# Where the weights of the 256-column products begin inside their tiles

## The chip, the cores and the metric

The kernel runs on one core of a Trainium2 chip. The metric is device time in microseconds of one execution, as the median of three runs; the two versions are compared by that time. The profile is of one further execution, recorded by the hardware profiler.

## What is computed

The reference is a two-layer trunk over 512 tokens of width 1024, with 256 memory tokens. Layer 0 mixes tokens by forgetting attention and differential attention, layer 1 by an mLSTM; each is followed by cross-attention to the memory and by a gated ConvFFN of inner width 2816. All is float32. The parts that matter here are the matrix products:

```python
def memory_cross_attention(xn, memn, wq, wkv, wo):
    q = split_heads(xn @ wq, XATTN_HEADS)
    k, v = jnp.split(memn @ wkv, 2, axis=-1)
...
def conv_ffn(xn, w_up, conv_w, conv_b, w_down):
    h = causal_depthwise_conv(xn @ w_up, conv_w) + conv_b
    g, u = jnp.split(h, 2, axis=-1)
    return (jax.nn.gelu(g) * u) @ w_down
...
    return rms_norm(x, final_norm)
```

## The kernel before

Activations stand transposed: a tile holds 128 features on the partitions and the 512 tokens along the free dimension. To keep float32 precision, each operand is split in two float32r parts, a high part (names ending in h: `xh`, `wh`, `ah`) made by ScalarE, and the rest (`xl`, `wl`, `al`) made by VectorE. One product of 128x128 weights with the columns is then three matmuls, `mm3` (lines 289 to 294): high weights on high columns (L292), high weights on low columns (L293), low weights on high columns (L294). Each matmul loads its own 128x128 weights first (the PEld rows of the profile) and then streams its columns.

Two widths of product occur. A wide one streams all 512 tokens. A narrow one streams 256 columns, and there are three kinds of it that take their weights from the tiles in question:

- The up-projection of the FFN (`seven`, for 21 of the 22 pairs of gate and value blocks in each layer) and the queries of the cross-attention (`p_query`, 4 per layer) are done by a scheme that replaces eight half products by seven, p1 to p7, each of four 128x128 weight blocks on 256 columns, so 84 matmuls for one pair. Their weights are `wh` and `wl` (sets f3 and f1, made by `parts`) and the smaller tiles `s2`, `s4`, `a22`, in which the high part takes 512 columns and the low part the next 512. Their columns come from `xh`/`xl` or from the sums kept in the `kv` tiles (`T1` to `T4`).
- The keys of the cross-attention (`p_proj` with n=MEM, and `p_fill`) stream the 256 memory tokens, tiles `mem`.
- The last three blocks of the last down-projection (`finish`, `part`) are done in two halves of 256 tokens each, so that the final norm of the first half can begin early. Their columns are `ah`/`al`.

A weight tile is 1088 columns wide for 1024 columns of weights, so the weights can begin up to 64 columns (256 bytes) into it. Where they begin is set by `OFF` for the narrow products, `parts(off)`:

```python
        return [self.til(self.wp, tag, (P, 1088), F32R, bufs=3)[:, off : off + 1024] for tag in ("wh", "wl")]
```

`OFF` is 16 columns, 64 bytes. The wide products of most projections begin at 0. The down-projection's wide products (`down`, through `block`) use `OFF` too, since their columns `ah`/`al` stand 64 bytes further than `xh`, `xl`, `kv` and `mem` do: the tile pools begin with pads (`pad`), and modulo 256 bytes the built program places `xh`, `xl`, `kv`, `mem` and the weight tiles at 96, and `ah`/`al` at 160. `finish` calls `weight` without an offset, so its weights begin at 0. The value projection with n=256 (`p_proj_tok`) has the roles exchanged: there the weight tile is what is streamed, and it begins 48 columns in; it is not touched.

Where a wide `down` or `plain` block is followed by a narrow product, the last 128 columns of its `wl` are put a further 16 columns in (32 for `plain` in layer 1): `d["step"]`, `b["step"]` and `low` in `block`. These steps are not touched either.

The order of the instructions is set by two planners, `Plan` (attention, memory, queries) and `Sched` (the FFN), from written-in costs. Neither looks at offsets, and TensorE takes its instructions in that order.

Of the kernel before, what the change touches and what calls it, by code (L numbers as in the profile page):

```python
# [17 lines left out]
P = 128  # L18
# [7 lines left out]
LAST = len(CHUNKS) - 1  # L26
# [12 lines left out]
PARTS = 3  # L39
BIG = 1e30  # L40

OFF = 16
BANKS = {"s": ("s", 2), "b": ("s", 2), "w": ("w", 2), "t": ("w", 2)}

FOX_Q, FOX_K, FOX_V, FOX_F, DIF_Q, DIF_K, DIF_V = 0, 512, 1024, 1536, 1544, 2056, 2568
# [21 lines left out]
class Plan:  # L67
# [11 lines left out]
    def add(self, fn, dur=0.0, deps=(), prio=None, take=(), free=(), chain=(), pre=(), after=0.0, order=(), load=(), st=None):  # L79
        it = Item(fn, dur, [d for d in deps if d is not None], len(self.items) if prio is None else prio, take, free, chain, pre, after, order, load, st)  # L80
        it.n = len(self.items)
        self.items.append(it)
        return it
# [154 lines left out]
class Builder:  # L238
# [868 lines left out]
    def p_fill(self, pl, layer, after, prio, blocks):  # L1107

        self.fills = []
        for b in range(blocks):  # L1110
            st = {}
            last = None
            for m in (2 * b, 2 * b + 1):
                for k in range(0, KB8, 4):

                    def fn(m=m, k=k, st=st):
                        if k == 0:
                            st["w"] = self.weight(self.t["xk"][layer, m], off=OFF)
                            if m % 2 == 0:
# [67 lines left out]
    def p_query(self, pl, layer, h, order):  # L1187
# [6 lines left out]
        def wide(tag, raw):  # L1194
            both = self.til(self.kp, tag, (P, 1088), F32R, bufs=1)
            s = st[tag] = [both[:, c : c + 512] for c in (OFF, OFF + 512)]
            self.split(*s, raw)
# [11 lines left out]
        def p1():  # L1209
# [5 lines left out]
            if h == 1:  # L1215
                self.rest_load(layer, 1)
            st["f3"] = self.parts(OFF)
            self.split(*st["f3"], st["raw"][:])
# [7 lines left out]
        def p5():  # L1226
            st["f1"] = self.parts(OFF)
            self.split(*st["f1"], self.sums[h][:])
            st["R"] = self.bank("s")
            product(st["f1"], 512, T1, "R", True, range(4 - (h == 0)))  # L1230
# [67 lines left out]
    def xattn(self, layer):  # L1298
        nc, t, tc = self.nc, self.t, self.tc
        with tc.tile_pool(name=f"xa{layer}", bufs=1, reuse_waits="tile") as mp:  # L1300
# [78 lines left out]
            for h in range(4):  # L1379
                p = 50 + 10 * h  # L1380
                ke = []
                for m in (2 * h, 2 * h + 1):
# [7 lines left out]
                    if m < 2 * len(self.fills):  # L1390
# [9 lines left out]
                        self.p_proj(  # L1400
                            pl, t["xk"][layer, m], self.mems, keys, kc, deps=[kvs], prio=p, n=MEM, per=4, off=OFF
                        )
# [118 lines left out]
    def ffn_steps(self, layer, mp):  # L1521
# [19 lines left out]
        def joined(deps, prio, free):  # L1541
            return add("-", 0.0, None, deps, prio, (), free, 0.0)
# [41 lines left out]
        def block(src, nk, xs, at, bank, deps, steps, tag="raw", off=0, onto=None):  # L1584

            st, lo = weight(src, nk * P, at, tag, off)
            last = None
            per = nk // steps

            def opened():  # L1590
                st["ps"] = self.bank(bank) if bank == "w" else self.acc_bank(st["_acc"] if bank == "acc" else 2 + st["_y"])

            if onto is not None:
                x, x_deps = onto

                def seed():
                    opened()
                    nc.scalar.copy(st["ps"][:], x[:])  # L1598

                last = add("ACT", act(512), seed, x_deps, at - 1.5, [(bank, st)])  # L1600
            for c in range(steps):

                def fn(c=c):
                    if c == 0 and onto is None:
                        opened()
                    for k in range(c * per, (c + 1) * per):
                        self.mm3(st["ps"][:], *st["rows"](k), *xs(k), k == 0 and onto is None, k == nk - 1, onto is not None)

                last = pe(0.7 * per, fn, [lo, last, *deps], [(bank, st)] if c == 0 and onto is None else (), [("h", st)] if c == steps - 1 else ())
            return st, last  # L1610
# [28 lines left out]
        def small_(tag):  # L1639
            both = self.til(self.kp, tag, (P, 1088), F32R, bufs=1)  # L1640
            return both[:, OFF : OFF + 512], both[:, OFF + 512 : OFF + 1024]

# [198 lines left out]
        def down(c, m, steps=1):  # L1841
            first, nk = CHUNKS[c]
            onto = (self.x[m], [xadded[m]]) if c < LAST and (c, m) not in ((0, 0), (0, 1)) else None
            d, last = block(
                t[f"down{c}"][layer, m], nk, lambda k: tuple(a[:] for a in acts[first + k]), clock[0], "w", [acted[first + k] for k in range(nk)], steps,
                "dr" if c < LAST else "raw", OFF, onto,
            )
            last.block, d["step"] = d, 16
            if m == 7:
                for k in range(nk):  # L1850
                    joined([last], last.prio, [("act", acted[first + k].st)])
            if onto is None:
                e = add("DVE", 0.6, lambda: self.xadd(m, d["ps"]), [last, xadded[m], *formed], clock[0] + 3.0, (), [("w", d)])
            else:
                e = add("ACT", act(512), lambda: nc.scalar.copy(self.x[m][:], d["ps"][:]), [last, *formed], clock[0] + 1.0, (), [("w", d)])
            xadded[m] = e
            return e

        def fill():
            nonlocal queue  # L1860
            if queue:
                down(*queue.pop(0))
# [15 lines left out]
        if layer == 0:  # L1878
            for m in range(8):
                e = down(LAST, m, 2)  # L1880
                a = add("ACT", 1.2, lambda m=m: self.xprep(m, "mix", 1, state), [e], clock[0] + 3.0)
                add("DVE", 1.3, None, [a], clock[0] + 3.0)
# [261 lines left out]
    def finish(self, mp, ah, al):  # L2144


        nc = self.nc
        nk = len(ah)
        wsrc = self.t[f"down{LAST}"][1]
        sq = self.til(self.sp, "sq", bufs=1)  # L2150
        HALF = [slice(0, 256), slice(256, 512)]
        outs = [self.til(self.kp, f"kv{i}", (P, 1024), F32R, bufs=1).bitcast(F32)[:, :512] for i in range(8)]

        def add(m, ps, c):
            x = self.x[m][:, c]
            nc.vector.tensor_tensor(out=x, in0=ps[:, c], in1=x, op=ALU.add)
            if m == 0:
                nc.scalar.activation(sq[:, c], x, AF.Square)
            else:
                end = m == 7 and c == HALF[1]  # L2160
                tmp = outs[0] if end else self.til(self.sp, "sqt")
                nc.scalar.activation(tmp[:, c], x, AF.Square)
                nc.vector.tensor_tensor(out=sq[:, c], in0=sq[:, c], in1=tmp[:, c], op=ALU.add)
            nc.scalar.activation(x, x, AF.Identity, scale=self.col("fin", m))

        def turned(h, n):

            t, f = 2 * h + n // 2, n % 2
            ps = banks[h][n]()
            for k in range(4 * f, 4 * f + 4):  # L2170
                nc.tensor.transpose(ps[:, k % 4 * P : k % 4 * P + P], self.x[k][:, t * P : (t + 1) * P], self.ident[:])
            return ps, t, f

        def write(ps, t, f, r, vector, own=False):
            out = outs.pop(0)
            if vector:
                nc.vector.tensor_scalar(out=out[:], in0=ps[:], scalar1=r, scalar2=None, op0=ALU.mult)
            else:
                nc.scalar.activation(out[:], ps[:], AF.Identity, scale=r)
            (nc.scalar if own else nc.sync).dma_start(self.t["y"][t][:, f * 512 : f * 512 + 512], out[:])  # L2180


        last = self.til(self.sp, "a", (P, 4))
        nc.scalar.activation(last[:], ah[-1][:, :4].bitcast(F32), AF.Sqrt, scale=0.0, bias=self.eps[:])
        for m in range(5):
            add(m, self.proj(wsrc[m], ah, al, nk=nk), slice(0, 512))
        w = [self.weight(wsrc[m], nk * P) for m in range(5, 8)]
        ps = [self.acc_bank(b) for b in range(3)]
        own = [lambda b=b: self.acc_bank(b) for b in range(4)]
        banks = [[own[3], lambda: self.bank("w"), lambda: self.bank("w"), lambda: self.bank("s")], own]  # L2190

        def part(m, c):
            for k in range(nk):
                s = slice(k * P, (k + 1) * P)
                self.mm3(ps[m - 5][:, c], w[m - 5][0][:, s], w[m - 5][1][:, s], ah[k][:, c], al[k][:, c], k == 0, k == nk - 1)
            add(m, ps[m - 5], c)

        r = []

        def norm(c):  # L2200
            r.append(self.rsqrt_last(sq[:, c], 256))

        for m in range(5, 8):
            part(m, HALF[0])
        part(5, HALF[1])
        norm(HALF[0])
        part(6, HALF[1])
        part(7, HALF[1])
        first = [turned(0, n) for n in range(4)]
        norm(HALF[1])  # L2210
        second = [turned(1, n) for n in range(4)]
        for n in range(4):
            write(*first[n], r[0][:, n // 2 : n // 2 + 1], n == 0)
        for n in range(4):
            write(*second[n], r[1][:, n // 2 : n // 2 + 1], n % 2, n == 2)
# [115 lines left out]
```

## Time and profile before

| what | value |
|---|---|
| median of 3 runs | 1452.01 us (1451.99 to 1452.08) |
| profiled execution | 1451.94 us |
| its span, first to last instruction | 1450.1 us |
| granted TensorE clock | 1.000 |
| PE busy, matmuls | 1435.6 us, 8971 |
| FFN of layer 0, about 412 to 707 us | PE busy 294.02 of 295.00 us |
| FFN of layer 1, about 1112 to 1415 us | PE busy 302.19 of 303.00 us |
| the end, 1415 to 1450 us | PE busy 28.83 of 35.00 us |

A matmul's time in the profile runs from its start until its last result is out, so it overlaps the next matmul: the mean duration of a row is not what one more matmul adds. That is the pace, the distance from one start to the next, which the timeline shows. For 256 columns a row of 276 ns goes with a pace of 113 ns.

### The profile page before, as it was taken

To read this page: it belongs to the slowest core of one execution; us is meant where nothing else is said; L and a number is where in the kernel's file an instruction comes from. 1 tells how busy PE (TensorE), PEld (TensorE's weight loads), DVE (VectorE), ACT (ScalarE), POOL (GpSimd) and SP (SyncE) were. 2 spreads that over 40 slices of the span, in tenths; PEclk is the share of its full clock that TensorE was granted. 3 is DMA by queue.
4 is the path that set the end of the run, shared out by engine and by line. 5 is a ranking of instruction groups with operands and counts; after the bars stand their busy time and mean duration, and the time that the engine had idled before them with its cause. 6 is when DMAs were issued, how large, how long until landed. Compare 5 with 4: busy or idle time off the path is not lost.

```text
span 1450.1 us, 24100 instructions
## 1 busy us (share of the span) xinstructions
PE 1435.6 (99%) x8971; PEld 1274.2 (88%) x8971; DVE 1226.5 (85%) x2199; ACT 1009.8 (70%) x1830; POOL 74.8 (5%) x116
## 2 busy tenths in 40 slices
PE   9999999999999999999999999999999999999998
PEld 7888788998889999999888788889988999999997
DVE  7789987877899988888689888887779999888875
ACT  7689766655678777777657676566566787777775
POOL 0001120000000000000000100000000000000000
PEclk9999999999999999999999999999999999999999
DMA  5222337652246665552233322656313666655312
GB/s 199 89 74 73 110 119 214 178 167 87 95 118 170 183 164 158 155 166 68 66 128 106 121 94 98 188 144 181 132 52 113 165 182 175 153 163 159 101 52 95
DMA packets 73367, 190.38 MB, mean 131 GB/s; under 512 B 8081, under 2 KB 10258, under 8 KB 73250
## 3 DMA queue, kind: packets, MB, share of 16 engines
q1 hardware_dynamic: 65474, 162.30, 33.6%
q0 software_dynamic: 7200, 26.22, 10.6%
q8 instruction: 70, 1.15, 0.3%
q14 instruction: 47, 0.39, 0.1%
q10 hardware_dynamic: 576, 0.33, 0.1%
HBM read 186.69 MB, written 2.13 MB: 130 GB/s over the span
## 4 chain that ended last, share of the span: by engine, by line
PE 80%; DVE 12%; ACT 4%; issue 2%; DMA 1%; POOL 0%; SPq 0%; DVEq 0%; ACTq 0%; POOLq 0%
PE acc L292 14%; PE acc L293 14%; PE acc L294 14%; PE w L294 6%; PE w L292 6%; PE w L293 6%; PE s L294 3%; PE s L292 3%; PE s L293 3%; DVE wl L283 3%; PE acc L353 2%; PE acc L355 2%; PE acc L354 2%; DVE c L1691 1%; DVE x L774 1%
## 5 line engine op out<-in xcount | busy, mean ns | idle before, releaser
L283 DVE TENSOR_TENSOR wl<-raw,wh 128x1024 fp32r<-128x1024 f32 (+2 forms) x181 | 209.4, 1157 | 37.5 <-ACT wh L286 29.0
L292 PE MATMUL acc<-xh,wh 128*128 128x256 f32 (+1 forms) x624 | 206.9, 332 | 0.2 <-ACT v L1932 0.2
L294 PE MATMUL acc<-xh,wl 128*128 128x256 f32 (+1 forms) x624 | 205.6, 329 | 0.1
L293 PE MATMUL acc<-xl,wh 128*128 128x256 f32 (+1 forms) x624 | 205.5, 329 | 0.0
L286 ACT CAST wh<-raw 128x1024 fp32r<-128x1024 f32 (+1 forms) x123 | 124.8, 1019 | 73.3 <-PE acc L293 35.7
L1691 DVE SCALAR_TENSOR_TENSOR c<-hs,vec,c 128x512 f32<-128x512 f32 x176 | 131.0, 747 | 14.6 <-ACT c L1684 12.6
L292 PEld LDWEIGHTS acc<-xh,wh 128*128 128x128 f32 x624 | 117.2, 188 | 12.8 <-ACT v L1932 0.9
L293 PEld LDWEIGHTS acc<-xl,wh 128*128 128x128 f32 x624 | 117.2, 188 | 12.2
L294 PEld LDWEIGHTS acc<-xh,wl 128*128 128x128 f32 x624 | 117.1, 188 | 12.1 <-DVE wl L283 0.7
L294 PE MATMUL w<-ah,wl 128*128 128x512 f32 x320 | 125.3, 392 | 0.0
L293 PE MATMUL w<-al,wh 128*128 128x512 f32 x320 | 124.8, 390 | 0.0
L292 PE MATMUL w<-ah,wh 128*128 128x512 f32 x320 | 124.8, 390 | 0.0
L1684 ACT ACTIVATE c<-hs,vec 128x512 f32<-128x512 f32 x88 | 71.2, 816 | 13.8 <-DVE hs L1831 7.4
L283 DVE TENSOR_TENSOR wl<-sa,wh 128x1024 fp32r<-128x1024 f32 x52 | 63.5, 1221 | 20.2 <-ACT wh L1762 18.5
L1568 ACT CAST wh<-dr 128x512 fp32r<-128x512 f32 (+1 forms) x80 | 46.0, 575 | 42.1 <-PE w L293 35.3
L294 PEld LDWEIGHTS w<-ah,wl 128*128 128x128 f32 x320 | 60.1, 188 | 12.7
L1762 ACT CAST wh<-sa 128x1024 fp32r<-128x1024 f32 x42 | 44.0, 1049 | 36.3 <-PE w L293 33.3
L292 PEld LDWEIGHTS w<-ah,wh 128*128 128x128 f32 x320 | 60.1, 188 | 10.3 <-ACT w L1598 0.2
L293 PEld LDWEIGHTS w<-al,wh 128*128 128x128 f32 x320 | 60.1, 188 | 10.1
L283 DVE TENSOR_TENSOR wl<-dr,wh 128x128 fp32r<-128x128 f32 (+3 forms) x148 | 55.6, 410 | 9.4 <-ACT wh L1568 9.3
L1747 POOL DMA_DIRECT2D sa<-in_up_dram x42 | 35.9, 855 | 514.8 <-DVE hs L1831 209.7
L283 DVE TENSOR_TENSOR s<-sb,s 128x512 fp32r<-128x512 f32 x88 | 60.2, 685 | 2.2
(571 smaller groups left out, 4656.1 us busy)
## 6 DMA issues: line engine op xcount, KB each, us to landing
raw<-in_up_dram SPq DMA_DIRECT2D x46, 512.0 KB, 3.2
sa<-in_up_dram SPq DMA_DIRECT2D x42, 512.0 KB, 3.4
sa<-in_up_dram POOLq DMA_DIRECT2D x42, 512.0 KB, 5.8
dr<-in_down_dram SPq DMA_DIRECT2D x64, 256.0 KB, 2.6
ra<-in_up_dram SPq DMA_DIRECT2D x42, 256.0 KB, 2.8
raw<-in_xk_dram SPq DMA_DIRECT2D x16, 512.0 KB, 3.3
raw<-in_wo_dram SPq DMA_DIRECT2D x16, 512.0 KB, 3.8
raw<-in_xv_dram SPq DMA_DIRECT2D x16, 512.0 KB, 3.3
```

The source lines that it names most:

```text
L283: self.nc.vector.tensor_tensor(out=lo, in0=v, in1=hi.bitcast(F32), op=ALU.subtract)
L286: self.nc.scalar.copy(hi, v)
L292: mm(out, wh, xh, start=first, stop=False, skip_group_check=parts)
L293: mm(out, wh, xl, start=False, stop=False, skip_group_check=parts)
L294: mm(out, wl, xh, start=False, stop=last, skip_group_check=parts)
L353: mm(ps, xh[k][:, ts], wh[:, ws], start=(k == 0), stop=False)
L354: mm(ps, xh[k][:, ts], wl[:, ws], start=False, stop=False)
L1568: nc.scalar.copy(st["wh"][:, :cols], st[tag][:, :cols])
L1684: nc.scalar.activation(st["c_"][:, j, :], hs()[:, j, 2:514], AF.Identity, scale=self.col("cw", (layer * 3 + 2) * 44 + blk), bias=self.col( ...
L1691: nc.vector.scalar_tensor_tensor(out=c, in0=hs()[:, j, n : n + 512], scalar=w, in1=c, op0=ALU.mult, op1=ALU.add)
L1747: return add("POOL", 0.0029 * cols, lambda: nc.gpsimd.dma_start(out(), src(), accum_op=ALU.add), deps, due, (), (), 6.0)
L1762: nc.scalar.copy(s["wh"][:, :cols], raw())
```

## The change

```diff
-OFF = 16
+OFF, DOWN = 32, 16
...
             d, last = block(
                 t[f"down{c}"][layer, m], nk, lambda k: tuple(a[:] for a in acts[first + k]), clock[0], "w", [acted[first + k] for k in range(nk)], steps,
-                "dr" if c < LAST else "raw", OFF, onto,
+                "dr" if c < LAST else "raw", DOWN, onto,
             )
...
-        w = [self.weight(wsrc[m], nk * P) for m in range(5, 8)]
+        w = [self.weight(wsrc[m], nk * P, OFF) for m in range(5, 8)]
```

`OFF` is used in `p_query`, `p_fill`, the keys' `p_proj`, and in `seven` (f3, f1, s2, s4, a22). All those weights now begin 32 columns, 128 bytes, into their tiles. The three narrow blocks of `finish` go from 0 to 128 bytes. The down-projection's wide blocks stay at 64 bytes under the name `DOWN`. No tile moves and none changes its size, and the instructions and their order on all five engines are the same as before: in the built programs, 4584 matmuls have their weights 64 bytes further, 72 have them 128 bytes further, and no streamed operand has another address.

## Prediction

> **What bounds the kernel now.** I read the page first. TensorE is busy for 99% of the span, at full clock, and the chain that ended last is TensorE's for 80%:
>
> ```profile
> PE 1435.6 (99%) x8971; PEld 1274.2 (88%) x8971; DVE 1226.5 (85%) x2199; ACT 1009.8 (70%) x1830; POOL 74.8 (5%) x116
> ...
> PEclk9999999999999999999999999999999999999999
> ...
> PE 80%; DVE 12%; ACT 4%; issue 2%; DMA 1%; POOL 0%; SPq 0%; DVEq 0%; ACTq 0%; POOLq 0%
> ```
>
> So a nanosecond more or less for each matmul shows nearly whole in the time. Next I read TensorE's groups with different shapes kept apart; the last number ahead of the idle time is the mean duration of one, in ns:
>
> ```profile
> L293 PE MATMUL acc<-xl,wh 128*128 128x256 f32 x336 | 93.0, 277 | 0.0
> L292 PE MATMUL acc<-kv,a 128*128 128x256 f32 x200 | 56.0, 280 | 1.6 <-DVE hs L1808 1.6
> L294 PE MATMUL acc<-kv,wl 128*128 128x256 f32 x200 | 55.3, 276 | 0.0
> L292 PE MATMUL acc<-mem,wh 128*128 128x256 f32 x128 | 36.3, 283 | 0.0
> L294 PE MATMUL acc<-mem,wl 128*128 128x256 f32 x128 | 35.9, 280 | 0.0
> L292 PE MATMUL w<-xh,wh 128*128 128x256 f32 x64 | 17.9, 280 | 0.0
> L294 PE MATMUL w<-xh,wl 128*128 128x256 f32 x64 | 17.8, 278 | 0.0
> L294 PE MATMUL s<-kv,xl 128*128 128x256 f32 x32 | 9.0, 282 | 0.0
> L292 PE MATMUL acc<-ah,wh 128*128 128x256 f32 x24 | 6.8, 283 | 0.0
> L293 PE MATMUL acc<-al,wh 128*128 128x256 f32 x24 | 6.7, 279 | 0.0
> ```
>
> The first two x200 rows are the slowest and one of the fastest of fifteen such groups (the seven products and the queries; their means average 277.2). With three groups each of x336, x64 and x128 these are 4584 matmuls whose weights the change moves by 64 bytes; the `ah`/`al` rows are the 72 of `finish`. The same shape takes from 276 to 283 ns. The timeline shows what that means. A quiet stretch of the queries in layer 0, where the two rows are 18 starts apart:
>
> ```profile
> 275.90 0.28 PE L293 MATMUL acc<-kv,a 128*128 128x256 f32 x1
> ...
> 277.94 0.28 PE L293 MATMUL s<-xl,s 128*128 128x256 f32 x1
> ```
>
> 2.04 us / 18 = 113.3 ns. The next pair, 5 us later, is 51 starts apart:
>
> ```profile
> 280.86 0.28 PE L294 MATMUL w<-xh,wl 128*128 128x256 f32 x1
> ...
> 286.87 0.28 PE L294 MATMUL acc<-kv,wl 128*128 128x256 f32 x1
> ```
>
> 6.01 / 51 = 117.8 ns, for the same kinds of product with the same addresses modulo 256 bytes. So there are two steady paces, and TensorE can stay in the slow one for long. Two kinds of product with other addresses show a third and a fourth case, the scores of layer 0 (8 starts) and `finish` (26 starts):
>
> ```profile
> 362.01 0.28 PE L294 MATMUL s<-kv,xl 128*128 128x256 f32 x1
> ...
> 362.97 0.28 PE L293 MATMUL s<-kv,xh 128*128 128x256 f32 x1
> ```
>
> ```profile
> 1430.93 0.28 PE L292 MATMUL acc<-ah,wh 128*128 128x256 f32 x1
> ...
> 1433.99 0.28 PE L294 MATMUL acc<-ah,wl 128*128 128x256 f32 x1
> ```
>
> 0.96 / 8 = 120.0 ns, and 3.06 / 26 = 117.7 ns.
>
> What separates them I call the distance: the address of the weights being loaded for the next matmul minus that of the columns being streamed meanwhile, modulo 256 bytes. From the tile addresses of the built program it is 64 in both query stretches (160 minus 96), 0 in the scores (96 minus 96), 192 in `finish` (96 minus 160). Distance 0 settles at 120.0, distance 192 stays at 117.7, and distance 64 has a free pace, 113.3, and a disturbed one, 117.8. My reading: the load of the next weights and the stream of the columns get in each other's way at certain meetings, and with so few columns to stream there is too little slack to hide it.
>
> **The change, part by part.** It adds and removes no instruction and moves none in the order; no wait, queue or transfer is touched, so each of these costs nothing. ScalarE and VectorE write the same number of columns 64 bytes further on; both engines have idle time (70% and 85% busy), and no row here shows a writing time that depends on the start, so I take nothing.
>
> *Distance 64 becomes 128* for nearly all of the 4584. No 256-column product of before has distance 128, so its pace must be bounded. From below by the free pace, 276 ns per row, since no steady pace in the trace is better: 3000 x 1.2 (the fifteen groups) + 1008 x 1 (x336) + 192 x 2.7 (x64, mean about 278.7) + 384 x 5.3 (x128, mean 281.3) = 3.6 + 1.0 + 0.5 + 2.0 = 7.1 us gained at most, and really less, since the means hold restarts after waits that stay. From above by the pace of the scores, 120.0, where a row takes 276 + 6.7 = 283: 3000 x 5.8 + 1008 x 6 + 192 x 4.3 + 384 x 1.7 = 17.4 + 6.0 + 0.8 + 0.7 = 24.9 us lost. The disturbed pace of 117.8 (281 ns) lies between: 11.4 + 4.0 + 0.4 - 0.1 = 15.7 us lost.
>
> Which is it nearest to? There is one clean look at distance 128, in a wide product. In layer 1 the last `wl` block of the `plain` pair is put 128 bytes further, and is loaded while `xl` streams; in layer 0 it is put 64 bytes further:
>
> ```profile
> 1114.07 0.39 PE L292 MATMUL acc<-xh,wh 128*128 128x512 f32 x1
> 1114.29 0.40 PE L293 MATMUL acc<-xl,wh 128*128 128x512 f32 x1
> 1114.53 0.40 PE L294 MATMUL acc<-xh,wl 128*128 128x512 f32 x1
> ```
>
> ```profile
> 414.66 0.39 PE L292 MATMUL acc<-xh,wh 128*128 128x512 f32 x1
> 414.89 0.39 PE L293 MATMUL acc<-xl,wh 128*128 128x512 f32 x1
> 415.11 0.40 PE L294 MATMUL acc<-xh,wl 128*128 128x512 f32 x1
> ```
>
> The second row of each is the matmul in question. With distance 64 the next start comes 0.22 us later, as in the undisturbed stream ahead of it (0.23); with distance 128 it comes 0.24 us later, and the matmul's own row is 0.01 us longer. Within the rounding of these rows that is the 6.7 ns by which 120.0 exceeds 113.3. A load at distance 128 that starts in the normal place thus holds up the stream beside it, and in a narrow product it should do so as well, as there too the next weights are loaded while the columns stream. A steady state can shift where the load starts and soften this, as the scores show, whose groups average 282 and not 283. I take 282: 3000 x 4.8 + 1008 x 5 + 192 x 3.3 + 384 x 0.7 = 14.4 + 5.0 + 0.6 + 0.3 = 20.3 us.
>
> *`finish` goes from distance 192 to 64* (224 minus 160). From 117.7 to at best 113.3: 72 x 4.4 = 0.3 us gained; at worst it enters the disturbed pace of distance 64, which costs the same as now, so nothing. I take 0.3.
>
> *Entries and waits.* The first narrow matmul after a down block has its weights loaded at distance 64 where it was 0. Some 70 entries of at most 9 ns each: 0.6 us either way, taken as nothing. Where TensorE waits for VectorE, a slower TensorE waits less:
>
> ```profile
> PE acc L292 <- DVE hs L1808: 1.6, 2, 0.8
> PE s L292 <- ACT xe L1234: 0.3, 1, 0.3
> ```
>
> These are the waits that narrow products show by name, so at most about 2 us comes back; I count 1.9.
>
> Sum: 1451.94 (the profiled execution: 1450.1 span and 1.8 around it; 0.07 under the median) + 20.3 - 0.3 - 1.9 = 1470.0 us. The bounds by the same sum are 1451.9 + 15.7 - 2.2 = 1465 and 1451.9 + 24.9 - 0.3 = 1476.5.
>
> **The rivals.**
>
> *Free pace at 128.* Distance 128 may turn out to have a steady place for the load in which nothing meets, and, unlike 64, no disturbed one. For it: the pace at 64 shows that such places exist, and the two stretches at 64 differ by no address, so a small shift of the load's start decides. Against it: the one look above, where the load cost about 0.01 us at once. It would give 1451.9 - 7.1 - 0.3 = 1444.5 at best, 1447 with the restarts left in. It decides from the point where the mean of the fifteen groups falls under 277. Chance 0.23.
>
> *The address has no say.* The paces would differ for another reason (how a stretch was entered, whether a wait came before it), and the change moves nothing: 1452. For it: both 113.3 and 117.8 occur at distance 64. Against it: `finish` and the scores have one pace throughout, and the two `plain` blocks differ by their step alone. Chance 0.15. The Trainium skill's page "TensorE: Matmul & The Clock Gate" (Part 2, "Step-by-step: what each phase is for") speaks for this rival: it gives TensorE two independent read ports, one for the streamed operand and one for weights, and says that loading the next weights takes no bandwidth from the running matmul. By that rule the sum would be 0. The trace does not agree where the rows above show 113.3, 117.7 and 120.0 ns for one shape at one clock.
>
> *The change does not do what it says.* If a tile base moved along, the distance would stay; but in the built programs only the weights' addresses differ. No chance of its own.
>
> *A later bound.* If TensorE slows by 20 us, nothing else becomes the bound, since all other engines gain slack.
>
> **How the numbers follow.** A disturbed pace at 128 (between 281 and 283 ns) has 0.62, the free pace 0.23, no effect 0.15. A measurement of this kernel can tell 0.2%, 2.9 us, from no change. The likeliest case gives 1470, its own range 1460 to 1478 (the low end if a third of the stretches find the free pace). The range that holds 8 in 10 must reach into the free pace: 1447 to 1478. Faster by over 0.2%: 0.22; within: 0.16; slower: 0.62.
>
> **What would show it.** Right: the fifteen x200 groups rise from 276 to 280 up to 280 to 283, alike in both layers; the pace in the FFN is 117 to 120 ns; the `ah`/`al` rows of 256 columns fall from 279 to 283 to about 276; wide rows stay at 390. Wrong: groups at 276 throughout (free pace), or a mix of 113.3 and 117.8 as now (no effect). If the wide rows change, the entries matter more than I allow.

## The result, and the profile after

The changed kernel takes 1468.26 us (median of 4 runs, 1467.08 to 1468.62), beside 1452.05 us (4 runs, 1451.99 to 1452.23) before: 1.0111 of the time, 95% interval 1.01 to 1.0123. That is 16.2 us slower; the forecast was 1470.0. The profiled execution took 1468.62 us, with a span of 1466.8 us.

The page's busy times, TensorE's clock and the engines' shares of the chain that ended last, after:

```profile
PE 1454.6 (99%) x8971; PEld 1295.0 (88%) x8971; DVE 1227.7 (84%) x2199; ACT 1012.1 (69%) x1830; POOL 74.2 (5%) x116
...
PEclk9999999999999999999999999999999999999999
...
PE 85%; DVE 8%; ACT 3%; issue 2%; DMA 1%; POOL 0%; DVEq 0%; SPq 0%; POOLq 0%; ACTq 0%
```

The instruction counts are those of before and the clock is full. TensorE is busy for 19.0 us more and its weight loads for 20.8 us more, while VectorE and ScalarE gain 1 to 2 us. TensorE's share of the chain rises from 80% to 85% and VectorE's falls from 12% to 8%: TensorE slowed down, and a part of the waits for VectorE went away.

TensorE's groups after, with shapes kept apart (busy us, mean ns of one, idle time before them):

```profile
L292 PE MATMUL w<-ah,wh 128*128 128x512 f32 x320 | 125.5, 392 | 0.0
L293 PE MATMUL w<-al,wh 128*128 128x512 f32 x320 | 124.9, 390 | 0.0
...
L293 PE MATMUL acc<-xl,wh 128*128 128x256 f32 x336 | 94.5, 281 | 0.0
L292 PE MATMUL acc<-kv,a 128*128 128x256 f32 x200 | 56.7, 283 | 0.0
...
L294 PE MATMUL acc<-kv,wl 128*128 128x256 f32 x200 | 56.3, 282 | 0.0
...
L292 PE MATMUL acc<-mem,wh 128*128 128x256 f32 x128 | 36.5, 285 | 0.0
...
L294 PE MATMUL acc<-mem,wl 128*128 128x256 f32 x128 | 36.1, 282 | 0.0
L292 PE MATMUL w<-xh,wh 128*128 128x256 f32 x64 | 18.1, 283 | 0.0
...
L292 PE MATMUL acc<-ah,wh 128*128 128x256 f32 x24 | 6.8, 283 | 0.0
L293 PE MATMUL acc<-al,wh 128*128 128x256 f32 x24 | 6.7, 280 | 0.0
```

The fifteen x200 groups now stand at 281 to 283 ns, mean 281.9, where they stood at 276 to 280. The x336 rows went from 277 to 281, the `mem` rows rose by 2. Most wide rows did not move (390), but `ah,wh` of the down blocks rose from 390 to 392. The `ah`/`al` rows of `finish`, which the forecast had falling to 276, stand at 283 and 280.

The timeline after, in the stretch of the queries in layer 0 that was looked at before. These two rows are 49 starts apart:

```profile
276.05 0.28 PE L293 MATMUL acc<-kv,a 128*128 128x256 f32 x1
...
281.87 0.28 PE L294 MATMUL w<-xh,wl 128*128 128x256 f32 x1
```

5.82 us / 49 = 118.8 ns. Before, the same products ran at 113.3 in one stretch and 117.8 in the next. In `finish` after, 27 starts apart:

```profile
1447.67 0.28 PE L292 MATMUL acc<-ah,wh 128*128 128x256 f32 x1
...
1450.85 0.28 PE L292 MATMUL acc<-ah,wh 128*128 128x256 f32 x1
```

3.18 / 27 = 117.8 ns, the disturbed pace of distance 64. The first 48 products of `finish` run like this; the last 24, behind a pause, run at 113.3 ns (the part on `finish` alone shows their rows).

Of the waits that TensorE shows by name, the row for `hs` at line 1808 (1.6 us before) is gone from `acc L292`; among those that remain are these two:

```profile
PE s L769 <- DVE sm L774: 1.5, 2, 1.1
...
PE s L292 <- ACT xe L1234: 0.3, 1, 0.3
```

All of it can be put into a sum from TensorE's starts. There are 4498 pairs of consecutive matmuls in which both are narrow and the second one's weights were moved. I call a pair that lasts over 125 ns a waiting pair and take the others as the pace. The pace is 114.22 ns before (4446 pairs) and 118.71 after (4469 pairs): 4498 x 4.49 = 20.2 us more. The waiting pairs held 7.9 us above the pace before (52 of them) and 3.4 after (29): 4.5 us given back. Pairs of two wide matmuls add 0.3 us, the steps from narrow to wide 0.3, and pairs with a matmul of another width 0.6; `finish`, the steps from wide to narrow and the narrow pairs whose weights stayed each take off 0.1. 20.2 - 4.5 + 0.3 + 0.3 + 0.6 - 0.3 = 16.6, and the spans differ by 16.7.

### The profile page after: what moved, and what is told of

The parts are those of the page before. It is cut to its first block, busy times and chain, and to the rows that moved or that the text cites. A ratio compares the mean times of both kernels' runs of the same rounds, so it can differ in the third digit from the quotient of the medians.

```text
span 1466.8 us, 24100 instructions
## 1 busy us (share of the span) xinstructions
PE 1454.6 (99%) x8971; PEld 1295.0 (88%) x8971; DVE 1227.7 (84%) x2199; ACT 1012.1 (69%) x1830; POOL 74.2 (5%) x116
## 4 chain that ended last, share of the span: by engine, by line
PE 85%; DVE 8%; ACT 3%; issue 2%; DMA 1%; POOL 0%; DVEq 0%; SPq 0%; POOLq 0%; ACTq 0%
PE acc L292 15%; PE acc L293 15%; PE acc L294 15%; PE w L292 6%; PE w L294 6%; PE w L293 6%; PE s L292 4%; PE s L294 4%; PE s L293 4%; PE acc L353 2%; PE acc L355 2%; PE acc L354 2%; DVE wl L283 1%; DVE x L774 1%; DVE cv L1962 1%
## 5 line engine op out<-in xcount | busy, mean ns | idle before, releaser
L283 DVE TENSOR_TENSOR wl<-raw,wh 128x1024 fp32r<-128x1024 f32 (+2 forms) x181 | 208.9, 1155 | 38.5 <-ACT wh L286 29.7
L292 PE MATMUL acc<-xh,wh 128*128 128x256 f32 (+1 forms) x624 | 208.4, 334 | 0.2 <-ACT v L1932 0.2
L294 PE MATMUL acc<-xh,wl 128*128 128x256 f32 (+1 forms) x624 | 207.1, 332 | 0.2 <-DVE wl L283 0.2
L293 PE MATMUL acc<-xl,wh 128*128 128x256 f32 (+1 forms) x624 | 207.1, 332 | 0.0
L292 PEld LDWEIGHTS acc<-xh,wh 128*128 128x128 f32 x624 | 117.3, 188 | 12.8 <-ACT v L1932 0.8
L293 PEld LDWEIGHTS acc<-xl,wh 128*128 128x128 f32 x624 | 117.4, 188 | 12.2
L294 PEld LDWEIGHTS acc<-xh,wl 128*128 128x128 f32 x624 | 117.4, 188 | 11.9 <-DVE wl L283 0.6
L294 PE MATMUL w<-ah,wl 128*128 128x512 f32 x320 | 125.5, 392 | 0.0
L292 PE MATMUL w<-ah,wh 128*128 128x512 f32 x320 | 125.5, 392 | 0.0
L293 PE MATMUL w<-al,wh 128*128 128x512 f32 x320 | 124.9, 390 | 0.0
L283 DVE TENSOR_TENSOR wl<-sa,wh 128x1024 fp32r<-128x1024 f32 x52 | 63.5, 1221 | 28.3 <-ACT wh L1762 26.2
L294 PEld LDWEIGHTS w<-ah,wl 128*128 128x128 f32 x320 | 60.1, 188 | 13.1
L292 PEld LDWEIGHTS w<-ah,wh 128*128 128x128 f32 x320 | 60.1, 188 | 10.4 <-ACT w L1598 0.2
L293 PEld LDWEIGHTS w<-al,wh 128*128 128x128 f32 x320 | 60.2, 188 | 10.2
L283 DVE TENSOR_TENSOR wl<-dr,wh 128x128 fp32r<-128x128 f32 (+3 forms) x148 | 55.5, 410 | 11.3 <-ACT wh L1568 11.0
L283 DVE TENSOR_TENSOR s<-sb,s 128x512 fp32r<-128x512 f32 x88 | 60.3, 685 | 2.1
```

Of the source, the lines that this page charges most:

```text
L283: self.nc.vector.tensor_tensor(out=lo, in0=v, in1=hi.bitcast(F32), op=ALU.subtract)
L292: mm(out, wh, xh, start=first, stop=False, skip_group_check=parts)
L293: mm(out, wh, xl, start=False, stop=False, skip_group_check=parts)
L294: mm(out, wl, xh, start=False, stop=last, skip_group_check=parts)
```

## The experiments

The theory is that of the prediction: the distance of the loading weights from the streaming columns, modulo 256 bytes, sets the pace of narrow products. Three rivals were tried against it. The address might count modulo 128 bytes, or the weights' start alone might count and not the distance (further in, slower), or the address might have no say and the pace follow from how a stretch is entered.

### The distance in steps

Seven kernels are the kernel before with `OFF` alone changed; the down blocks and `finish` keep the addresses of before. The edit of the first, whose weights begin at the start of their tiles:

```diff
-OFF = 16
+OFF, DOWN = 0, 16
...
-                "dr" if c < LAST else "raw", OFF, onto,
+                "dr" if c < LAST else "raw", DOWN, onto,
```

The other six have 12, 17, 20, 24, 48 and 64 in place of 0. What was expected at distance 0 (`OFF` 0), 48 (12), 68 (17), 80 (20), 96 (24), 192 (48) and 256 (64), in this order:

> OFF is 0, the down blocks stay at 64 bytes, finish as before. Theory: distance 0, pace 118.5 to 120 as the scores, 4498 x (118.5 - 114.2) = 19 us and up to 26 us, 1469 to 1477. Rival (modulo 128): 0 is the same as 128, so the 1468 of the change. Rival (the further in, the slower): not over 1452.

> OFF is 12 columns (48 bytes), the down blocks at 64 bytes, finish as before: the other side of distance 64. If the free pace is a narrow place around 64, 48 is as slow as 80 (118.7 ns, 1468); if only a weight start on a 64-byte step has it, the same; if the place is broad on this side, 1452 or less.

> OFF is 17 columns (68 bytes), one column past before: how narrow the free pace is. Narrow place of less than a column: 1460 to 1470 and no starts at 113.3 ns in a row. Wider than a column: 1450 to 1455.

> OFF is 20 columns (80 bytes), the down blocks at 64 bytes, finish as before: a search for a place with a free pace and no disturbed one. Between distance 64 (1452) and 96 (1464). If the free pace is a narrow place: 1455 to 1464. If it is broad: 1452 or, without the disturbed stretches, down to 1447.

> OFF is 24 columns (96 bytes), half way between before and the change; the rest as in dist0. Theory gives no pace for distance 96, only that it has one of its own: 1446 (free pace everywhere) to 1476 (120 ns everywhere). If only 64-byte steps count, it falls on 1452 or on 1468.

> OFF is 48 columns (192 bytes), the down blocks stay at 64 bytes, the three narrow blocks of finish at 0 as before. Theory (the distance between the loaded weights and the streamed columns, modulo 256 bytes, sets the pace): distance 192, whose only pace in the trace of before is 117.7 ns, so 4498 x (117.7 - 114.2) = 15.7 us over before, 1466 to 1468, and 281 ns in the x200 groups. Rival (only the distance modulo 128 bytes counts): 192 is the same as 64, so 1452 and groups of 276 to 280. Rival (the further in, the slower): over 1468.

> OFF is 64 columns (256 bytes), the rest as in dist0. Theory with a period of 256 bytes: the same time as dist0 within 1 us. If the period is longer, or the place inside the tile counts by itself: another time, by the rival of the place slower than all others.

Measured; the pace is the mean of the same 4498 pairs, those over 125 ns left out:

| distance, bytes | us, median | ratio to before, 95% | pace, ns |
|---|---|---|---|
| 0 | 1474.48 | 1.0138 to 1.0168 | 119.8 |
| 48 | 1466.24 | 1.0076 to 1.0109 | 117.9 |
| 64 (before) | 1452.05 | | 114.2 |
| 68 | 1467.49 | 1.0087 to 1.0117 | 118.3 |
| 80 | 1467.76 | 1.0094 to 1.0124 | 118.7 |
| 96 | 1464.00 | 1.0064 to 1.0095 | 117.7 |
| 128 (the change) | 1468.26 | 1.01 to 1.0123 | 118.7 |
| 192 | 1462.65 | 1.0056 to 1.0086 | 117.7 |
| 256 | 1474.59 | 1.0134 to 1.0167 | 119.8 |

At 48 and at 68 some of the pairs left out are no waits: 190 pairs of 130 ns and 49 of 126 ns recur there. With them the pace is 118.4 at both. Two of the times miss what was expected: 80 lies above its 1455 to 1464, and 192 below its 1466 to 1468.

The groups at distance 0:

```profile
L293 PE MATMUL acc<-xl,wh 128*128 128x256 f32 x336 | 95.1, 283 | 0.0
...
L292 PE MATMUL acc<-kv,a 128*128 128x256 f32 x200 | 56.8, 284 | 0.0
L294 PE MATMUL acc<-kv,wl 128*128 128x256 f32 x200 | 56.8, 284 | 0.0
```

At distance 256, where the weights sit 256 bytes further on than at 0:

```profile
L293 PE MATMUL acc<-xl,wh 128*128 128x256 f32 x336 | 95.1, 283 | 0.0
...
L292 PE MATMUL acc<-kv,a 128*128 128x256 f32 x200 | 56.8, 284 | 0.0
L294 PE MATMUL acc<-kv,wl 128*128 128x256 f32 x200 | 56.8, 284 | 0.0
```

And at distance 192:

```profile
L293 PE MATMUL acc<-xl,wh 128*128 128x256 f32 x336 | 93.8, 279 | 0.0
L292 PE MATMUL acc<-kv,a 128*128 128x256 f32 x200 | 56.4, 282 | 0.2
...
L294 PE MATMUL acc<-kv,wl 128*128 128x256 f32 x200 | 55.8, 279 | 0.0
```

0 and 256 agree in time and in every row of the products whose weights moved, which is what a period of 256 bytes gives. A period of 128 is refuted, since 0 (119.8 ns) differs from 128 (118.7), and 64 (114.2) from 192 (117.7). "Further in is slower" falls too: 192 is faster than 128, and 256 is as slow as 0. And the address has a say: one number changes in the code, the order of the work doesn't, and the time moves by 22 us. Of the distances tried only 64 has the free pace for most of the time. Distance 192 has it in one place of each layer, in the keys that follow the products `s<-kv,qh`. These two rows of layer 0 are 23 starts apart:

```profile
317.71 0.28 PE L292 MATMUL acc<-mem,wh 128*128 128x256 f32 x1
...
320.32 0.28 PE L294 MATMUL acc<-mem,wl 128*128 128x256 f32 x1
```

2.61 / 23 = 113.5 ns. The products `s<-kv,qh` just ahead have the same addresses, at distance 64, in all kernels of the table. Yet they run at 113.3 to 113.5 ns when the distance of the others is 80, 96 or 192, and at 117.7 to 117.8 when it is 0, 48, 64, 68 or 256; at 128 they change over on the way. So at one distance what runs ahead can choose the pace. The keys that follow lose a free pace at once at 80 (118.8 ns), 96 (120.1) and 128 (118.3, behind starts of 112 to 114): a free entry does not help there.

At 68, one column beyond 64, the free pace is already lost:

```profile
L293 PE MATMUL acc<-xl,wh 128*128 128x256 f32 x336 | 94.5, 281 | 0.0
L292 PE MATMUL acc<-kv,a 128*128 128x256 f32 x200 | 56.6, 283 | 0.1
...
L294 PE MATMUL acc<-kv,wl 128*128 128x256 f32 x200 | 56.2, 281 | 0.0
```

The times come out below what the pace alone gives, as in the change: at 192, 4498 x 3.5 = 15.7 us by the pace, and 11.4 by the span of the same execution (1461.5 beside 1450.1). Slower products leave fewer and shorter waits.

### Moving the columns and not the weights

If the distance counts, and not where the weights begin, moving the streamed columns must do the same as moving the weights the other way. The tiles `kv` are streamed in most of the x200 groups. One kernel is the changed one with `kv` 64 bytes further on, which brings those products back to distance 64; `SMALL` keeps the weights in `s2`, `a22` and `s4`, which move with `kv`, at the addresses of the change:

```diff
+SMALL = 16
...
+            self.pad(self.kp, 64)
             self.kv = [self.til(self.kp, f"kv{i}", (P, 1024), F32R, bufs=1) for i in range(8)]
...
-            self.pad(self.kp, 128)
+            self.pad(self.kp, 64)
...
-            s = st[tag] = [both[:, c : c + 512] for c in (OFF, OFF + 512)]
+            s = st[tag] = [both[:, c : c + 512] for c in (SMALL, SMALL + 512)]
...
-            return both[:, OFF : OFF + 512], both[:, OFF + 512 : OFF + 1024]
+            return both[:, SMALL : SMALL + 512], both[:, SMALL + 512 : SMALL + 1024]
```

> The change, with the kv tiles themselves 64 bytes further (a pad of 64 bytes ahead of them, 64 less behind; s2, a22 and s4 take 16 columns less inside their tiles, so that all weights stay exactly where the change has them). Products that stream kv (T1 to T4, 2334 pairs) are back at distance 64, those that stream xh, xl and mem stay at 128; the weights' own places are the change's in both. Theory: the acc<-kv and s<-kv rows fall to 276 to 280 ns, the xh and mem rows stay at 281 to 285; 1468.3 - 2334 x (118.7 - 113.8) = 1457. Rival (the weights' place inside the tile counts by itself): all rows as in the change, 1468.

The other has the same pads on the kernel before, with `SMALL = 0`, so that no weights move and the `kv` products go from distance 64 to 0:

> The kernel before with the kv tiles 64 bytes further and the weights where before has them. Products that stream kv go to distance 0, the others stay at 64. Theory: kv rows rise to 282 to 284, xh rows stay at 276 to 278; 1452.1 + 2334 x (119.8 - 113.8) = 1466. Rival (the weights' place by itself): nothing moves, 1452.

Measured: 1464.34 us (1.0071 to 1.0101 of before) for the first, and 1463.53 (1.0064 to 1.0098) for the second. The groups of the first; its lines are numbered one higher:

```profile
L294 PE MATMUL acc<-xl,wh 128*128 128x256 f32 x336 | 94.5, 281 | 0.0
L293 PE MATMUL acc<-kv,a 128*128 128x256 f32 x200 | 56.5, 283 | 0.6 <-DVE hs L1810 0.6
...
L295 PE MATMUL acc<-kv,wl 128*128 128x256 f32 x200 | 55.4, 277 | 0.0
L293 PE MATMUL acc<-mem,wh 128*128 128x256 f32 x128 | 36.4, 285 | 0.0
```

And of the second:

```profile
L294 PE MATMUL acc<-xl,wh 128*128 128x256 f32 x336 | 93.2, 277 | 0.0
L293 PE MATMUL acc<-kv,a 128*128 128x256 f32 x200 | 56.8, 284 | 0.5 <-DVE hs L1810 0.5
...
L295 PE MATMUL acc<-kv,wl 128*128 128x256 f32 x200 | 56.4, 282 | 0.0
```

In the first, `kv,wl` falls from 282 to 277, and the products that stream `xl` or `mem` stay as in the change. The row `kv,a` of L293 stays at 283, the only one of the twelve `kv` groups that doesn't fall; by the starts, the pairs behind it go from 118.6 to 117.1 ns. In the second, `kv,a` and `kv,wl` rise to 284 and 282 with their weights where they were, and `xl` keeps its 277. All 4498 pairs say the same: the 2334 that stream `kv` go from 118.8 to 115.9 ns in the first and from 113.7 to 118.9 in the second, while the others stay at 118.6 to 118.7 in the first and go from 114.7 to 115.1 in the second. So it is the distance: both ways of changing it act on the products whose distance changes, and on the others hardly at all. The second came nearer to its expectation (1466) than the first (1457), which got back only about 4 of the 11 us. Its pace shows where the rest is: its pairs at distance 64 average 115.9 ns and not 113.7, because over half of their stretches stay at the disturbed pace. They are entered from products at 128, which may be why; the last kernel below bears on that.

### `finish` alone

The kernel before with only the last three blocks moved, from distance 192 to 64:

```diff
-        w = [self.weight(wsrc[m], nk * P) for m in range(5, 8)]
+        w = [self.weight(wsrc[m], nk * P, 32) for m in range(5, 8)]
```

> The kernel before with the change in finish alone: its three narrow blocks begin at 128 bytes, distance 64 in place of 192. As on record: 0.3 us gained if they reach the free pace, ah/al rows of 256 columns at 276. After the profile of the change: they enter the disturbed pace of distance 64 and stay there, rows at 279 to 283, within 0.2 us of before.

Measured: 1452.51 us (10 runs) beside 1452.11, ratio 0.9993 to 1.0012. Its groups:

```profile
L292 PE MATMUL acc<-ah,wh 128*128 128x256 f32 x24 | 6.8, 283 | 0.0
...
L293 PE MATMUL acc<-al,wh 128*128 128x256 f32 x24 | 6.7, 280 | 0.0
```

The timeline of `finish` there, 44 starts apart:

```profile
1431.04 0.28 PE L292 MATMUL acc<-ah,wh 128*128 128x256 f32 x1
...
1436.22 0.28 PE L294 MATMUL acc<-ah,wl 128*128 128x256 f32 x1
```

5.18 / 44 = 117.7 ns. It has the right distance, and the first 48 of its 72 products never reach the free pace. The last 24 come behind a pause for the sums of the norm (L477) and reach it; these two rows are 18 starts apart:

```profile
1437.66 0.28 PE L294 MATMUL acc<-ah,wl 128*128 128x256 f32 x1
...
1439.70 0.28 PE L294 MATMUL acc<-ah,wl 128*128 128x256 f32 x1
```

2.04 / 18 = 113.3 ns. The trace of the change shows the same two parts. In the first kernel with `kv` moved, with `finish` at distance 64 as well, the last 24 stay at 117.7 behind the same pause.

### The wide down blocks at 128

The change leaves the down blocks where they are (distance 0 to their columns). This kernel is the one before with them at distance 128, to see whether 512 columns hide the load:

```diff
-OFF = 16
+OFF, DOWN = 16, 48
...
-                "dr" if c < LAST else "raw", OFF, onto,
+                "dr" if c < LAST else "raw", DOWN, onto,
```

> The kernel before with the wide blocks of the down-projection alone at 192 bytes into their tiles, so that their distance (columns at 160 modulo 256) is 128 in place of 0; the narrow products as before. It tests the step of the prediction that a load at distance 128 holds up the stream beside it also where 512 columns leave slack. If it does as in the one look (about 7 ns each): 820 pairs x 7 = 5.7 us, 1458, w<-ah,wh rows at 394 to 397. If part of it is taken up by a shift as in the narrow products (4.5 ns): 3.7 us, 1456. Rival (slack in the wide products hides the load): 1452, rows at 390.

Measured: 1456.45 us, 1.0016 to 1.004 of before. The three groups:

```profile
L294 PE MATMUL w<-ah,wl 128*128 128x512 f32 x320 | 126.9, 396 | 0.0
L293 PE MATMUL w<-al,wh 128*128 128x512 f32 x320 | 126.1, 394 | 0.0
L292 PE MATMUL w<-ah,wh 128*128 128x512 f32 x320 | 125.7, 393 | 0.0
```

They stood at 390 to 392 before, and the 820 pairs whose distance went from 0 to 128 go from 228.1 to 231.9 ns. A wide matmul doesn't hide a bad distance, but it pays 3.8 ns, a little over half of the 6.7 ns that the prediction read into the one look in `plain`.

### Everything at 64

If 64 is the best place, a kernel in which all products have it could beat both. It also undoes the two special steps of the down blocks. Its edit, cut to the numbers:

```diff
-OFF = 16
+OFF, DOWN = 16, 32
...
-    def weight(self, src, cols=1024, off=0):
+    def weight(self, src, cols=1024, off=OFF):
...
-        wh, wl = self.weight(src, nk * P)
+        wh, wl = self.weight(src, nk * P, DOWN)
...
-                    st["w"] = ready if ready and c == 0 else self.weight(src[c], off=0 if n == 512 else 48)
+                    st["w"] = ready if ready and c == 0 else self.weight(src[c], off=48)
...
-                last.block, b["step"] = b, (16, 32)[layer]
+                last.block, b["step"] = b, 0
...
-            last.block, d["step"] = d, 16
+            last.block, d["step"] = d, 0
...
-        w = [self.weight(wsrc[m], nk * P) for m in range(5, 8)]
+        w = [self.weight(wsrc[m], nk * P, DOWN) for m in range(5, 8)]
```

> A search for a version that beats both: the wide products too at distance 64. Projections, plain blocks and values begin so many columns in that their distance is 64 in place of 0 (16 columns, 48 where the weight tile is what streams, 32 for everything that meets ah/al), finish too, and the steps of 16 and 32 columns for a last wl block are set to 0. Theory, if distance 64 is the free place for wide products as for narrow ones: the 72 wide pairs that had it in before went at 226.2 ns and the 2929 at distance 0 at 228.0, so 2929 x 1.8 = 5.3 us less, 1447. If wide products at 64 have a disturbed state as narrow ones do, or if the entries without the steps leave narrow stretches disturbed (4500 x 3.5 ns at most): 1452 to 1468.

Measured: 1466.47 us, 1.008 to 1.0113 of before. Its groups:

```profile
L294 PE MATMUL w<-ah,wl 128*128 128x512 f32 x320 | 126.7, 396 | 0.0
...
L293 PE MATMUL acc<-xl,wh 128*128 128x512 f32 x288 | 114.0, 396 | 0.0
L293 PE MATMUL acc<-xl,wh 128*128 128x256 f32 x336 | 94.1, 280 | 0.0
...
L292 PE MATMUL acc<-kv,a 128*128 128x256 f32 x200 | 56.0, 280 | 1.6 <-DVE hs L1808 1.6
...
L292 PE MATMUL acc<-ah,wh 128*128 128x256 f32 x24 | 6.7, 280 | 0.0
L293 PE MATMUL acc<-al,wh 128*128 128x256 f32 x24 | 6.6, 276 | 0.0
```

The hope of 1447 fell, and the other case that was named, 1452 to 1468, came true. Wide products lose at 64: the undisturbed ones of 2983 pairs average 233.2 ns, where they had 228.0 at distance 0, more than at 128 (231.9). So in a steady stream the better place for 512 columns is 0, and for 256 columns it is 64, while 0 is their worst. Here too it matters what runs ahead: before, 72 wide pairs at 64, single ones among pairs at 0, took 226.2 ns. The narrow products changed as well, though the addresses of most didn't: `xl,wh` at 256 columns went from 277 to 280, and the narrow pairs at 64 average 116.1 ns. What changed for those is what comes ahead of them (and the order of 58 of the 8971 matmuls). And `finish`, at the same distance 64 as in the change, now runs freely; 33 starts apart:

```profile
1450.23 0.28 PE L292 MATMUL acc<-ah,wh 128*128 128x256 f32 x1
...
1453.97 0.28 PE L292 MATMUL acc<-ah,wh 128*128 128x256 f32 x1
```

3.74 / 33 = 113.3 ns, and the wide blocks ahead of it run 10 starts in 2.34 us:

```profile
1446.63 0.40 PE L293 MATMUL acc<-al,wh 128*128 128x512 f32 x1
...
1448.97 0.40 PE L294 MATMUL acc<-ah,wl 128*128 128x512 f32 x1
```

That is 234 ns each. Entered from wide products at distance 64, `finish` found the free pace at once. Entered from wide products at distance 192 (229 ns each), as in the kernel with `finish` alone, its first 48 products did not. The rival in which the entry decides is thus right in part: the distance says which paces there are, and where there are two, at 64 and in one place at 192, what ran ahead chooses. What it is about the entry that chooses is not shown: the pause inside `finish` led to either pace.

No kernel of the series beats the one before.

## Why the prediction was right

**The mechanism held.** The time rose because narrow products at distance 128 have no free pace, even where they are entered from one. The series shows it by one number, the two kernels with `kv` moved show that it is the distance, and TensorE's starts put 20.2 us on these pairs, beside the 20.3 forecast. The chosen row of 282 ns, between the disturbed pace (281) and the scores (283), was measured as 281.9 in the fifteen groups. That it came so near is in part luck: 282 was read from the scores, which are at distance 0, and the products in question stand at 283 to 284 when they are at 0.

**The waits were mis-sized.** The term of 1.9 us counted two waits that narrow products show by name. It left out two more of the same view, `s L293 <- DVE kv L283` (0.4 us) and `s L294 <- DVE wl L283` (0.2). And TensorE's starts held 7.9 us in 52 waiting pairs, of which 4.5 came back. These 2.6 us more than explain the 1.7 us by which the forecast came out high; the two terms below took a part of them off again.

**`finish` was mis-sized.** The term took 0.3 us as gained and named the other case (nothing) as its bound. The result lies near the bound, 0.1 us: in the run with it alone and in the trace after, 48 of the 72 products stay at the disturbed pace and the last 24 become free.

**What the prediction took as nothing** came to 1.1 us: the entries from wide to narrow took off 0.1, well inside the 0.6 either way that it allowed, but wide pairs, steps from narrow to wide and pairs of other widths added 1.2. The largest part of it among the wide pairs is `ah,wh` of the down blocks, 228.0 to 229.8 ns in 318 pairs, 0.6 us. Their addresses did not change; why they slowed was not followed up. The prediction had the wide rows staying at 390, and named a change in them as a sign that entries matter more than it allowed.

**The one look was weaker evidence than it was made.** The prediction read the price of a load at 128 from one wide matmul, 0.24 beside 0.22 us. The steady price of 128 in wide products is 3.8 ns, and in narrow ones 5.4 (118.7 beside 113.3), where the prediction read 6.7 into the look; and at 64, where the one look showed no price at all, wide products in a steady stream pay 5 ns. A single load that starts in the place of its predecessor's stream tells little about the place where the stream settles. The forecast was saved by the rows of the scores, a steady stream.

**Of the rivals,** the free pace at 128 is refuted (fifteen groups at 281 to 283), and "the address has no say" is refuted by the series. One argument against the latter was weaker than it looked, that `finish` has one pace throughout: at its distance of 192 the free pace occurs as well. The Trainium skill's page "TensorE: Matmul & The Clock Gate" (Part 2, "Step-by-step: what each phase is for") says that loading the next weights takes no read bandwidth from the running matmul. The rule that the prediction drew from it, a sum of 0, does not hold for these products: by address alone their pace moved from 114.2 to 119.8 ns. Whether read bandwidth is what they lose, no run shows.

**What stays open.** The runs show which distances cost time and how much, not what it is that load and stream meet at. Why 256 columns are best at 64 and 512 at 0, and why a stretch at 64 enters one pace or the other, was not settled.

## What to carry to other kernels

When a matmul's row differs between groups of the same shape, take the start-to-start pace and set it against the addresses of the next weights and of the streamed columns, modulo 256 bytes, before looking for a wait. Tune the distance for each width by itself, in a steady stream and not from one matmul, and measure the neighbours too, since the pace carries over from one stretch to the next. And when TensorE slows down evenly, count on small waits giving back a part: here 4.5 of 20.2 us, more than the listed waits show.

## What the runs showed of the hardware

The free place is narrow: at 256 columns, distance 64 has a pace of 113.3 ns and 68 averages 118.4 with the recurring pairs of 126 ns. The cost repeats after 256 bytes (119.8 at 0 and at 256). At one distance and one clock there can be two steady paces, 113.3 and 117.8 ns at 64, and the products ahead can choose between them; at 192 the free one was seen in one place of each layer only, at 128 not at all. And the best distance depends on the width: 64 for 256 columns, and in steady streams 0 for 512 (228.0 ns, beside 231.9 at 128 and 233.2 at 64).
